# Tying the woven projections and the score products to each other in the third attention unit

## The chip, the cores and the metric

The kernel runs on one core of one Trainium2 chip. The metric is the device time of one execution in microseconds (us). It is given as the median of three executions; the profile is of one further execution.

## The reference, cut to what matters

The reference is a two-layer diffusion backbone over 1024 latent tokens (a grid 64 wide) and 256 context tokens, 1024 features wide. The even layer, in which the change lies, projects the normalised tokens to queries, keys, values and gates, and attends in two groups of eight heads with two key heads each:

```python
for i in range(DEPTH):                      # DEPTH = 2
    h_lat = rms_norm(x_lat, norm_g[i]) * (1 + sc_l) + sh_l      # h_ctx likewise
    if i % 2 == 0:
        # A: all 1280 keys, normalised q and k, rotary;  B: keys within 128 and the context, a sink
        oa, ob = softmax(qa @ ka.T) @ va, softmax(qb @ kb.T + band) @ vb
        y_lat = concat([oa * silu(ag), ob * silu(bg)]) @ w_out
    else:
        y_lat = ...                         # convolution and neighbourhood attention
    x_lat = x_lat + g_l * y_lat
return rms_norm(x_lat, final_g)
```

## The kernel before, in words

Every product is kept near 32-bit accuracy by splitting both operands into a high and a low part: `mm3` (L317) makes three matmuls of one, high by high, high by low and low by high, and leaves the last of them in `done[0]` (L315). Weights are loaded raw, cast to their high part on ScalarE (ACT) and subtracted to their low part on GpSimd (POOL) in `load_w` (L324); the loads are issued by SyncE (SP), two raw buffers deep.

The attention of the even layer is cut into four **units** of one key head and four query heads. `ORDER` (L76) runs them as 2, 3, 0, 1: two of group B with 42 tiles each, then two of group A with 84 each. A unit has ten blocks of 128 queries, in the order `QORD`; a **tile** is one block against 128 keys. The generator `attn_gen` (L392) makes the tiles of all units one after the other, in two steps a tile. The first step traces two score products `st` (L465 with the queries' high part, L469 with the low part and the row maxima), an exponential `pf` on ACT (L477), its cast `ph` on ACT and the rest `pl` on POOL or VectorE (DVE) (L296, L299). The second flushes the tile three before: three products `ov` with the values (L409 to L411). Scores have two PSUM banks and `pf` two buffers. Before a block's first tile can be completed, its row maxima are needed: products `mx` (L576, L588) that DVE reduces (L578, L589), a transpose `trn` (L387) and the write of `QL` (L388). The high part of a unit's keys comes back from DRAM (`KAt`, L551) and ACT copies it into the lower operand (`KBt`, L555).

Beside the attention of one unit runs the projection of the next. `fill0` (L865) gives the query, key and value products `pq` of `proj_qkv` (L789): ten blocks of 128 tokens, eight feature blocks of three matmuls with 384 columns each. It yields after feature blocks 1, 4 and 7, so that one **step** is six or nine matmuls. A block's result is copied from PSUM to `pc` on ACT (L802); two blocks share a `pc` buffer, of which there are three (`PCB`). Normalisation and rotary follow on ACT, DVE and POOL, and `qk_tail` (L834) transposes the result (`trk`, L838) and writes queries and keys to DRAM. A tail is taken up with a later block, or in one of the last four steps. `proj_gate` (L767) then makes the gate products `pg`, six results in eighteen steps. It uses the same eight weight buffers as `pq`, and its results the same two PSUM banks. The products `po` of the output projection (L1003) are the work beside the fourth unit; their inputs and weights need buffers that the gate products read last.

`weave` (L495) draws the two strands together. It takes one step of `main` after the other and, in proportion, the steps of `fill`. What it traces is not the order on the chip: a scheduler orders every engine's instructions by a timeline of its own, taking what is ready there and, among that, the lowest priority number. A fill step is traced with its number raised by 80 (`FL`, L502). With `lag`, every TensorE instruction of the step gets an edge behind an earlier score product, the one at `sts[-lag]` (L503): an edge of `issue_after` fixes the order on that one engine and adds no wait for the result. The order so found is fixed on the chip.

The third unit is loop index `k = 2` in L883 to L890. Its 168 main steps are woven in two calls: 120 steps with 34 steps of `fill0(3)` (30 of `pq` and four of tails), then 48 steps with 18 of `proj_gate`. In the kernel before, `lag` is used in the odd layer alone (L1505 to L1512).

Of the kernel before, what the change touches and what calls it, by code (L numbers as in the profile page):

```python
# [49 lines left out]
NLAST = (48, 28)  # L50
# [16 lines left out]
ENDS = ((0, 0, 512), (1, 0, 256), (1, 256, 256))  # L67
LATE = 100
NFILL = (34, 34, 34)
HV = (('gggvvvvg',) * 3, ('gggvvvvg', 'vvvgvvvg', 'gggvvvvg'))  # L70
O1 = (6, 84, 46, 14)
TICK0, TICK1 = (1, 3)
# [3 lines left out]
ORDER = (2, 3, 0, 1)  # L76
# [11 lines left out]
def tile_kernel(ctx: ExitStack, tc: tile.TileContext, a, out):  # L88
    nc = tc.nc
    VE, SC, GP, PE, SY = nc.vector, nc.scalar, nc.gpsimd, nc.tensor, nc.sync  # L90
# [8 lines left out]
    turn = [0, 0]  # L99
    mk, mwp, hold, layer = [0], [None], [0], [0]  # L100
    sts, pvs = [], []

    def bank(tag, name):
        if tag == "pp" and solo[0]:
            turn[0] += 1
            tag = ("pp", "mx")[turn[0] // 2 % 2]
        return ps.tile([P, 512], F32, tag=tag, name=name, bufs=BUFS[tag])
# [3 lines left out]
    def nm(s):  # L111
        uid[0] += 1
        return f"{s}_{uid[0]}"
# [187 lines left out]
    def make_h(l, c, xs, bc, h):  # L301

        cond = 1 if c == 0 else 0
        for dk in range(DK):
            x = xs(dk)
            VE.scalar_tensor_tensor(x, x, gs[l][:, dk, cond : cond + 1], bc, op0=ALU.mult, op1=ALU.mult)
            shift = modT[l][:, dk, cond : cond + 1]
            if HV[l][c][dk] == "v":
                SC.activation(h[0][:, dk, :], x, AF.Identity, bias=shift)
# [2 lines left out]
                SC.activation(x, x, AF.Identity, bias=shift)  # L312
                split(x, h[0][:, dk, :], h[1][:, dk, :])

    done = [None]  # L315

    def mm3(o, lh, ll, rh, rl, first, last):  # L317
        PE.matmul(o, lh, rh, start=first, stop=False)  # L318
# [73 lines left out]
    def attn_gen(pool, groups, vshare, look, nexts=None):  # L392
# [43 lines left out]
        def prepare(x, n):  # L436

            while n and work and work[0][0] <= x:
                if next(work[0][1], work) is work:
                    work.pop(0)  # L440
                else:
                    n -= 1
# [7 lines left out]
        for x, (g, t) in enumerate(items):  # L450
            if x + AHEAD < len(items):
                items[x + AHEAD][0].ahead(items[x + AHEAD][1])
            if t == 0:
                g.start()
                while any(p is g.prep for _, p in work):
                    prepare(len(items), 1)
                for k in g.ids:
                    next(preps[k])
                    work.append((x + LEAD[layer[0]], preps[k]))
            rate = g.rate * max(len(work), 1)  # L460
            k, q0, n, extra = g.tiles[t]
            KA, KB = g.k()
            st = bank("st", nm("st"))
            cs = slice(k * P, (k + 1) * P)
            sts.append(PE.matmul(st[:, :n], KA[:, cs], g.QH[:, q0 : q0 + n], start=True, stop=False))  # L465
            if not g.bias:
                for lhs, rhs in extra():
                    PE.matmul(st[:, :n], lhs, rhs, start=False, stop=False)
            PE.matmul(st[:, :n], KB[0:68, cs], g.QL[0:68, q0 : q0 + n], start=False, stop=True)  # L469
            ph = pool.tile([P, 512], F32R, tag="ph", name=nm("ph"), bufs=look + 1)  # L470
            pl = pool.tile([P, 512], F32R, tag="pl", name=nm("pl"), bufs=look + 1)
            pf = pool.tile([P, 512], F32, tag="pf" if layer[0] else "ost", name=nm("pf"), bufs=PFB)
            if g.bias and extra is not None:
                VE.tensor_tensor(pf[:, :n], st[:, :n], extra(), op=ALU.add)
                SC.activation(pf[:, :n], pf[:, :n], AF.Exp)
            else:
                SC.activation(pf[:, :n], st[:, :n], AF.Exp, scale=1.0 if g.bias else SCALE)  # L477
            cnt[0] += 1
            split(pf[:, :n], ph[:, :n], pl[:, :n], "s", "v" if cnt[0] % vshare == 0 else "g")
            pend.append((g, t, ph, pl))  # L480
            if t == len(g.tiles) // 2:
                g.gate()
            if t == len(g.tiles) - 1:
                g.last()
            prepare(x, rate // 2)
            yield
            if len(pend) > look:
                flush()
            prepare(x, rate - rate // 2)
            yield  # L490
# [1 line left out]
            flush()  # L492
            yield

    def weave(main, nmain, fill, nfill, last=True, all_fill=True, lag=0):  # L495

        done = 0
        for k in range(nmain):
            next(main, None)
            while done * nmain < (k + 1) * nfill:  # L500
                with ExitStack() as cx:
                    cx.enter_context(later(FL[layer[0]]))  # L502
                    if lag and len(sts) >= lag:  # L503
                        cx.enter_context(tc.issue_after(sts[-lag].ins))
                    next(fill, None)
                done += 1
        if all_fill:
            for _ in fill:
                pass
        if last:  # L510
            for _ in main:
                pass
# [139 lines left out]
    with ExitStack() as p0x:  # L652
# [114 lines left out]
        def proj_gate(u, ms):  # L767

            if u not in gw:
                gw[u] = load_g0(u) if u == ORDER[0] else load_w0("ev_g", u, 256)  # L770
            wh, wl = gw[u]
            for m, c in ms:
                t0, n = CHUNKS[c]
                pp = bank("pp", nm("pg"))
                for dk in range(DK):
                    ms_ = slice(m * P, (m + 1) * P)
                    mm3(pp[:, :n], wh[dk][:, ms_], wl[dk][:, ms_], Hs(h, 0, t0, n, dk), Hs(h, 1, t0, n, dk),
                        dk == 0, dk == DK - 1)
                    if dk % 3 == 1:
                        tick()  # L780
                        yield
                sg = ap.tile([P, 640], F32, tag="rt2", name=nm("sg"), bufs=2)
                silu2(pp[:, :n], sg[:, :n])
                mark[0] = SY.dma_start(Gs[u][:, m, t0 : t0 + n], sg[:, :n])
                for _ in range(2):
                    if tails:
                        qk_tail(*tails.pop(0))
# [71 lines left out]
        def gblocks(k):  # L859

            if k:
                return [], [(m, c) for c in range(3) for m in range(2)]
            return [(0, c) for c in range(3)], [(1, c) for c in range(3)]

        def fill0(k, w=None):  # L865
            yield from proj_qkv(ORDER[k], w)
            while tails and k:
                qk_tail(*tails.pop(0))
                yield
            yield from proj_gate(ORDER[k], gblocks(k)[0])  # L870
# [11 lines left out]
        main = attn_gen(a0, [group0(u, qb) for u in ORDER for qb in QORD], VS0, LOOK0)  # L882
        for k in range(3):  # L883
            u = ORDER[k]
            n = NSTEP[u // 2] + (12 if k == 0 else 0)
            n0 = 0 if k else N0
            if not k:
                weave(main, n0, proj_gate(u, gblocks(k)[1]), 9, False)
            weave(main, n - n0 - NLAST[u // 2], fill0(k + 1), NFILL[k], False)
            weave(main, NLAST[u // 2], proj_gate(ORDER[k + 1], gblocks(k + 1)[1]), 18, False)  # L890
        run(mods)


# [205 lines left out]
    with ExitStack():  # L1099
# [404 lines left out]
        main = attn_gen(dpool, groups1, VSH, LOOK1, {11: [], 12: [13, 14], 13: [15]})  # L1504
# [129 lines left out]
```

## Time and profile before

| what | value |
| --- | --- |
| median of three executions | 1556.66 us (1556.37 to 1558.11) |
| profiled execution, its own time | 1555.72 us |
| its span, first to last instruction | 1553.9 us |
| TensorE (PE) busy | 1449.1 us, 93% of the span |
| VectorE (DVE), GpSimd (POOL), ScalarE (ACT) busy | 1123.3, 833.5, 759.8 us |
| mean granted TensorE clock | 0.967 |

The span leaves out 1.8 us of the execution's own time that lie around it. In the profile's rows a line number like L465 is one of the kernel's source, names like `pq<-wh,hh` are the tile written and the tiles read, and PE stands for TensorE's matmuls, PEld for its weight loads. Matmuls are pipelined: one of 384 columns is shown with 0.34 us, though the next one starts sooner, so neighbouring rows overlap. A row's bracket gives the idle time of the engine before it and what ended it. In a table by stretches of time each row has the stretch, its length, the busy time and count of each engine, the granted clock, and the share and rate of the DMA engines.

### The profile page before, as it was taken

The numbers are of one execution on the slowest core, as the hardware profiler recorded it, in microseconds if no ns is written. First come the engines' busy times: TensorE is split into PE (matmuls) and PEld (weight loads), VectorE is DVE, ScalarE is ACT, GpSimd is POOL, SyncE is SP. The second block draws the span as 40 slices with busy tenths as digits, with TensorE's granted clock in tenths as the row PEclk, the third lists the DMA queues.
The fourth block names the chain that finished last, engine by engine and source line by source line (L and its number), as shares of the span: only waits on it lengthen the run. The fifth ranks groups of instructions, "written<-read, shape, count | busy, mean of one in ns | idle before, by whom it ended". The sixth has DMA issues, their size and how long they took to land.

```text
span 1553.9 us, 22052 instructions
## 1 busy us (share of the span) xinstructions
PE 1449.1 (93%) x6984; PEld 1172.3 (75%) x6984; DVE 1123.3 (72%) x2172; ACT 759.8 (49%) x1545; POOL 833.5 (54%) x762
## 2 busy tenths in 40 slices
PE   6989989999999989899999889999999999799995
PEld 1878868887789678678887668888787787687784
DVE  4998898689858666654577677999755457586776
ACT  2721354445454755565455555443434455545563
POOL 1561464555555676675455666664542443545574
PEclk9999999999999999999999999999999999899996
DMA  9548245423441124631111121213456888788623
GB/s 339 194 146 270 79 125 174 147 64 121 151 129 44 54 89 143 207 115 56 42 45 35 68 95 57 80 63 123 158 178 222 272 225 263 221 264 240 192 92 109
DMA packets 185614, 221.01 MB, mean 142 GB/s; under 512 B 17421, under 2 KB 139481, under 8 KB 185497
## 3 DMA queue, kind: packets, MB, share of 16 engines
q1 hardware_dynamic: 178832, 208.03, 43.1%
q10 hardware_dynamic: 6664, 11.57, 2.3%
q8 instruction: 55, 0.90, 0.2%
q14 instruction: 63, 0.51, 0.1%
HBM read 159.51 MB, written 60.03 MB: 141 GB/s over the span
## 4 chain that ended last, share of the span: by engine, by line
PE 67%; DVE 12%; DMA 11%; issue 3%; POOL 3%; ACT 2%; SPq 2%; DVEq 0%; ACTq 0%; POOLq 0%
PE p L320 6%; PE p L318 6%; PE p L319 6%; PE ov L409 4%; PE ov L410 4%; PE ov L411 4%; PE st L465 4%; PE po L318 4%; PE st L469 4%; PE po L319 4%; PE po L320 4%; PE pq L320 2%; PE pq L319 2%; PE pq L318 2%; DMA mw<-in_mod_w_dram 2%
## 5 line engine op out<-in xcount | busy, mean ns | idle before, releaser
L299 POOL TENSOR_TENSOR pl<-pf,ph 128x512 fp32r<-128x512 f32 (+4 forms) x321 | 399.9, 1258 | 270.7 <-ACT ph L296 218.9
L299 POOL TENSOR_TENSOR wl<-wr,wh 128x256 fp32r<-128x256 f32 (+2 forms) x256 | 197.7, 788 | 227.9 <-ACT wh L296 203.3
L477 ACT ACTIVATE pf<-st 128x512 f32<-128x512 f32 x284 | 166.2, 596 | 161.7 <-PE st L469 106.3
L296 ACT CAST ph<-pf 128x512 fp32r<-128x512 f32 (+4 forms) x364 | 209.2, 588 | 25.5 <-PE ov L410 17.6
L296 ACT CAST wh<-wr 128x256 fp32r<-128x256 f32 (+2 forms) x264 | 103.2, 404 | 172.2 <-DMA wr<-in_od_d_dram 39.3
L318 PE MATMUL p<-hh,wh 128*128 128x512 f32 x448 | 177.7, 399 | 3.7 <-DVE spk L299 1.4
L319 PE MATMUL p<-hl,wh 128*128 128x512 f32 x448 | 177.9, 398 | 0.2 <-POOL hl L299 0.2
L320 PE MATMUL p<-hh,wl 128*128 128x512 f32 x448 | 175.2, 399 | 0.1
L465 PE MATMUL st<-QH,KAt 128*128 128x512 f32 (+4 forms) x364 | 144.0, 397 | 19.8 <-ACT pf L477 16.5
L409 PE MATMUL ov<-ph,Vt 128*128 128x512 f32 (+4 forms) x364 | 143.6, 394 | 8.8 <-DVE y L631 6.4
L411 PE MATMUL ov<-pl,Vt 128*128 128x512 f32 (+4 forms) x364 | 143.7, 395 | 3.9 <-POOL pl L299 3.8
L410 PE MATMUL ov<-ph,Vt 128*64 128x512 f32 (+4 forms) x364 | 140.8, 387 | 0.0
L469 PE MATMUL st<-QL,KBt 68*128 68x512 f32 (+4 forms) x364 | 138.2, 388 | 0.8 <-DVE QL L388 0.7
L1116 DVE SCALAR_TENSOR_TENSOR cps<-U,taps,cps 128x512 f32<-128x512 f32 x184 | 124.3, 747 | 0.0
L589 DVE TENSOR_REDUCE mp<-mx 128x1 f32<-128x512 f32 x128 | 85.5, 682 | 33.5 <-PE mx L588 32.7
L219 DVE SCALAR_TENSOR_TENSOR macc<-mw,csil,macc 128x512 f32<-128x512 f32 x107 | 97.5, 929 | 14.0 <-DMA mw<-in_mod_w_dram 13.2
L318 PEld LDWEIGHTS p<-hh,wh 128*128 128x128 f32 x448 | 84.6, 189 | 24.5 <-DVE spk L299 1.6
L465 PEld LDWEIGHTS st<-QH,KAt 128*128 128x128 f32 x364 | 69.8, 192 | 42.5 <-ACT pf L477 25.3
L319 PEld LDWEIGHTS p<-hl,wh 128*128 128x128 f32 x448 | 84.6, 189 | 20.4 <-POOL hl L299 0.6
L320 PEld LDWEIGHTS p<-hh,wl 128*128 128x128 f32 x448 | 84.6, 189 | 20.3 <-POOL wl L299 1.0
L411 PEld LDWEIGHTS ov<-pl,Vt 128*128 128x128 f32 x364 | 71.1, 195 | 28.1 <-POOL pl L299 7.6
L409 PEld LDWEIGHTS ov<-ph,Vt 128*128 128x128 f32 x364 | 71.5, 196 | 24.3 <-issue 7.0
(277 smaller groups left out, 3518.4 us busy)
## 6 DMA issues: line engine op xcount, KB each, us to landing
mw<-in_mod_w_dram SPq DMA_DIRECT2D x34, 512.0 KB, 5.6
bs<-in_d_bs_dram SPq DMA_DIRECT2D x16, 832.0 KB, 7.3
Q<-qs SPq DMA_DIRECT2D x40, 256.0 KB, 2.7
QH<-Q SPq DMA_DIRECT2D x80, 128.0 KB, 2.7
bm<-in_d_bm_dram SPq DMA_DIRECT2D x16, 540.0 KB, 6.1
wr<-in_od_d_dram SPq DMA_DIRECT2D x64, 128.0 KB, 2.6
mw<-in_mod_w_dram SPq DMA_DIRECT2D x28, 256.0 KB, 3.1
wr<-in_ev_qkv_dram SPq DMA_DIRECT2D x32, 192.0 KB, 3.8
```

Source lines behind the costliest of these rows:

```text
L296: SC.copy(hi, src)
L299: (GP if leng == "g" else VE).tensor_tensor(lo, src, hi.bitcast(F32), op=ALU.subtract)
L318: PE.matmul(o, lh, rh, start=first, stop=False)
L319: PE.matmul(o, lh, rl, start=False, stop=False)
L320: done[0] = PE.matmul(o, ll, rh, start=False, stop=last)
L409: PE.matmul(o, V[:, 64:192], ph[:, :n], start=(t == 0), stop=False)
L410: PE.matmul(g.ov[0:64, q0 : q0 + n], V[:, 0:64], ph[:, :n], start=False, stop=False)
L411: pvs.append(PE.matmul(o, V[:, 64:192], pl[:, :n], start=False, stop=(last and g.sink is None)))
L465: sts.append(PE.matmul(st[:, :n], KA[:, cs], g.QH[:, q0 : q0 + n], start=True, stop=False))
L469: PE.matmul(st[:, :n], KB[0:68, cs], g.QL[0:68, q0 : q0 + n], start=False, stop=True)
L477: SC.activation(pf[:, :n], st[:, :n], AF.Exp, scale=1.0 if g.bias else SCALE)
L1116: VE.scalar_tensor_tensor(pc, uc, w, pc, op0=ALU.mult, op1=ALU.add)
```

## The change

In the third unit alone, both calls of `weave` get `lag=4` and a new `tie=2`. With `lag`, every PE instruction of a fill step is ordered behind the fourth-last score product traced so far. With `tie`, `weave` notes after each fill step the last `mm3` product traced (`prods` is another name for the list `done`, since `done` is a local counter in `weave`), and the L465 product of the next tile is ordered behind the product noted two fill steps back in the same call. No operation, buffer or transfer is added or removed.

```diff
+HOLD, TIE = 4, 2
...
+    tied = [None]
...
-    done = [None]
+    done = prods = [None]
...
-            sts.append(PE.matmul(st[:, :n], KA[:, cs], g.QH[:, q0 : q0 + n], start=True, stop=False))
+            with ExitStack() as cx:
+                if tied[0] is not None:
+                    cx.enter_context(tc.issue_after(tied[0].ins))
+                sts.append(PE.matmul(st[:, :n], KA[:, cs], g.QH[:, q0 : q0 + n], start=True, stop=False))
...
-    def weave(main, nmain, fill, nfill, last=True, all_fill=True, lag=0):
+    def weave(main, nmain, fill, nfill, last=True, all_fill=True, lag=0, tie=0):
 
         done = 0
+        past = []
         for k in range(nmain):
+            tied[0] = past[-tie] if tie and len(past) >= tie else None
             next(main, None)
+            tied[0] = None
             while done * nmain < (k + 1) * nfill:
                 with ExitStack() as cx:
                     cx.enter_context(later(FL[layer[0]]))
                     if lag and len(sts) >= lag:
                         cx.enter_context(tc.issue_after(sts[-lag].ins))
                     next(fill, None)
+                past.append(prods[0])
                 done += 1
...
-            weave(main, n - n0 - NLAST[u // 2], fill0(k + 1), NFILL[k], False)
-            weave(main, NLAST[u // 2], proj_gate(ORDER[k + 1], gblocks(k + 1)[1]), 18, False)
+            hold = dict(lag=HOLD, tie=TIE) if k == 2 else {}
+            weave(main, n - n0 - NLAST[u // 2], fill0(k + 1), NFILL[k], False, **hold)
+            weave(main, NLAST[u // 2], proj_gate(ORDER[k + 1], gblocks(k + 1)[1]), 18, False, **hold)
```

## The prediction

> **What bounds the kernel now.** The page comes first: which engine is busy, and whose work makes up the chain that ended last.
>
> ```profile
> span 1553.9 us, 22052 instructions
> ...
> PE 1449.1 (93%) x6984; PEld 1172.3 (75%) x6984; DVE 1123.3 (72%) x2172; ACT 759.8 (49%) x1545; POOL 833.5 (54%) x762
> ...
> PE 67%; DVE 12%; DMA 11%; issue 3%; POOL 3%; ACT 2%; SPq 2%; DVEq 0%; ACTq 0%; POOLq 0%
> ```
>
> PE leads both. The change takes no work from it, so it can win only where PE stands idle or runs at a lower clock. I therefore asked for a table by stretches from the end of the second unit's gate products to late in the fourth unit, cut where the products beside the attention begin or stop. The figures are the stretch, its length, the busy time of PE, PEld, DVE, ACT and POOL, the clock and the DMA share.
>
> ```profile
> core 0: us, PE busy (x) PEld busy (x) DVE busy (x) ACT busy (x) POOL busy (x), PEclk, DMA share, GB/s
> 437.20:485.10 47.90, 47.23 (x247) 41.69 (x247) 31.02 (x60) 24.27 (x47) 27.45 (x22) 1.00 0.30 95
> 485.10:503.00 17.90, 17.90 (x92) 15.95 (x92) 15.93 (x23) 10.56 (x19) 13.39 (x10) 1.00 0.12 37
> 503.00:544.50 41.50, 37.95 (x166) 26.64 (x165) 25.39 (x49) 29.14 (x52) 28.79 (x23) 1.00 0.17 54
> 544.50:556.00 11.50, 11.50 (x63) 10.84 (x63) 9.57 (x18) 5.67 (x12) 9.99 (x9) 1.00 0.26 85
> 556.00:580.20 24.20, 19.35 (x75) 13.50 (x74) 13.95 (x27) 13.97 (x28) 15.25 (x14) 0.86 0.27 80
> 580.20:640.00 59.80, 59.80 (x297) 48.46 (x296) 40.29 (x71) 34.29 (x62) 40.82 (x29) 1.00 0.44 136
> 640.00:669.40 29.40, 23.53 (x92) 16.16 (x91) 18.39 (x35) 18.93 (x33) 20.21 (x16) 0.94 0.89 281
> 690.00:860.00 170.00, 169.88 (x809) 136.80 (x808) 109.92 (x198) 85.37 (x162) 94.35 (x81) 1.00 0.16 48
> ```
>
> I call the first stretch A, the third B, the fifth C and the seventh D. PE idles 0.67 us in A, 3.55 in B, 4.85 in C and 5.87 in D, and not at all in the others before D. The clock costs at most 24.20 x 0.14 = 3.4 us in C and 29.40 x 0.06 = 1.8 in D. About 20 us are thus open. The last row is the pattern to reach: with `po` products mixed in, PE is idle for 0.12 of 170 us. The same stretches for tile `pq` alone (first figure: PE) tell why B is not like that:
>
> ```profile
> 437.20:485.10 47.90, 28.07 (x136) 23.99 (x136) 2.38 (x5) 1.00 0.30 95
> 485.10:503.00 17.90, 11.18 (x53) 9.41 (x52) 0.49 (x1) 1.00 0.12 37
> 503.00:544.50 41.50, 1.07 (x5) 0.91 (x5) 0.86 (x2) 1.00 0.17 54
> 544.50:556.00 11.50, 9.36 (x48) 8.35 (x48) 0.00 (x0) 1.00 0.26 85
> ```
>
> Most of the 240 `pq` matmuls run before 503; then 41 us of attention stand alone.
>
> **The change part by part.** *The hold moves `pq` out of A.* First, how far it runs ahead now: the L465 row for the time up to 471.3 and for 437.2 to 471.3, and three PE rows.
>
> ```profile
> L465 PE MATMUL st<-QH,KAt x84: 388/396/792, 159.4 to 470.3; 128*128 128x512 f32 x84
> ```
>
> ```profile
> L465 PE MATMUL st<-QH,KAt x12: 388/394/496, 442.2 to 470.3; 128*128 128x512 f32 x12
> ```
>
> ```profile
> 437.26 0.34 PE L318 MATMUL pq<-wh,hc 128*128 128x384 f32 x1
> 437.44 0.34 PE L319 MATMUL pq<-wl,hc 128*128 128x384 f32 x1
> ```
>
> ```profile
> 485.11 0.62 PE L469 MATMUL st<-QL,KBt 68*128 68x512 f32 x2
> ```
>
> Two units have 84 tiles, so the third unit's scores begin after 470.3 and its first two are completed at 485.11; `pq` starts at 437.26, ahead of 12 more scores of the second unit. With the change, step f of 34 is traced at main step 120f/34 and ordered behind the score four back: steps 0, 1, 2, 3 behind tiles -3, -2, 0, 2 of the unit. With two score banks, tile 2's product needs tile 0 completed. So at most steps 0 to 2, 24 matmuls, can run in A; 112 leave it. At the start-to-start time of 0.175 us (0.34 is a pipelined duration) that is 19.6 us of PE work, and 47.23 - 19.6 = 27.6 us remain. Does anything else hold A open? The unit's keys must arrive (ACT's row) and its maxima be reduced (tile `mp`, 449 to 478, DVE first):
>
> ```profile
> 448.48 1.26 ACT L555 CAST KBt<-KAt 64x1280 fp32r<-64x1280 f32 x1 [2.86 <-DMA KAt<-K]
> ```
>
> ```profile
> 449.00:478.00 29.00, 6.95 (x11) 0.00 (x0) 1.00 0.23 73
> ```
>
> The copy ends 12.5 us into A and the reductions need 7: 19.5 us, under the 27.6 of work. But in its fixed order ACT waits 2.86 us for that DMA with the exponentials queued behind, and `pq` covers this today. The nearest rows for attention alone are B, idle for 3.55/41.50 = 8.6%, a piece of the second unit, 2.90/28.00 = 10.4%, and C, 20%, where ACT also waits for a DMA:
>
> ```profile
> 344.00:372.00 28.00, 25.10 (x115) 17.54 (x114) 25.45 (x61) 17.81 (x41) 15.25 (x13) 1.00 0.31 92
> ```
>
> I take C's share: 5.5 us, so **+4.8** beside the 0.67 of now, and D's clock loss, **+1.8**. The ends are -0.7 (no idle left) and +19.6 (A as long as now).
>
> ```profile
> PE st L465 <- ACT pf L477: 1.2, 2, 0.8
> ```
>
> Here a rule of the Trainium skill can be weighed. C's clock fell after a hole of 2.19 us (row below), B's 3.55 us in smaller pieces (those of L465: 1.2 us in two) left it at 1.00. The Trainium skill, "TensorE: Matmul & The Clock Gate", Part 1, says that the clock halves after a window of about 3.4 us without work. By that rule A's short waits would cost no clock and the sum below would be 1.8 us lower; the trace's hole was shorter than that window and the clock fell.
>
> *The same matmuls fill B: **-3.6**.* From the third unit's start a step of 1.05 or 1.6 us (six or nine times 0.175) goes with every 1.76 tiles, and the tie keeps it from falling more than two steps behind, as in the row 690 to 860. What `pq` results cost elsewhere comes along: on tile `pc`, DVE, ACT and POOL work for 10.28, 5.67 and 3.77 us between 437.2 and 503.
>
> ```profile
> 437.20:503.00 65.80, 0.49 (x3) 0.39 (x3) 10.28 (x12) 5.67 (x12) 3.77 (x5) 1.00 0.25 79
> ```
>
> Even all of it on top of B's 25.39, 29.14 and 28.79 stays below B's length, which the moved `pq` makes longer still; the writes of queries, keys and values go with it on SP, behind which the next loads queue, and I count nothing for them. Lower and upper end: -3.6 and 0.
>
> *C.* PE, then ACT, in C; below, the same hand-over in the first and second unit:
>
> ```profile
> 560.61 0.50 PE L465 MATMUL st<-QH,KAt 128*128 128x512 f32 x1 [2.19 <-ACT pf L477]
> ...
> 572.77 0.49 PE L838 MATMUL trk<-ident,pc 128*128 128x128 f32 x3
> ...
> 580.21 0.28 PE L318 MATMUL pg<-hc,wh 128*128 128x256 f32 x1
> ```
>
> ```profile
> 559.14 0.40 ACT L296 CAST wh<-wr 128x256 fp32r<-128x256 f32 x1 [4.23 <-DMA wr<-in_ev_g_dram]
> ...
> 568.48 0.41 ACT L296 CAST wh<-wr 128x256 fp32r<-128x256 f32 x1 [0.62 <-DMA wr<-in_ev_g_dram]
> ...
> 577.80 0.88 ACT L802 COPY pc<-pq 128x384 f32<-128x384 f32 x2
> ```
>
> ```profile
> 225.00:238.00 13.00, 10.64 (x45) 7.55 (x44) 11.33 (x29) 10.01 (x28) 9.04 (x10) 0.87 0.51 159
> 384.00:394.00 10.00, 7.98 (x39) 5.74 (x39) 9.82 (x18) 5.29 (x15) 5.72 (x6) 1.00 0.41 123
> ```
>
> The last two `pq` blocks are finished by 556, but copied only at 577.80, after a tail's transposes at 572.77: they wait for a `pc` buffer, and the gate, which needs their banks, starts at 580.21. Its weights were ready by 568.9. Spread out, `pq` ends behind tile 48 and before 53, its tails in step with it, and the gate starts from tile 57 on. What then remains is the weight loading, as in the earlier hand-overs: 2.36 us idle with 1.7 of clock, and 2.02 idle; 3 in the middle. From 4.85 + 3.4 to 3: **-5.2**, with ends 0 and -8.2. The ties add an order, no semaphore: if the gate's weights are late, the score of tile 62 and every `mx` and `ov` behind it wait in PE's queue. From 556 to 568.9 the loads took 13 us; nine tiles lie between, at B's 41.50/24 = 1.73 us (48 score products, two a tile) 15.6 us. I take nothing; if that cover goes, up to 4.
>
> ```profile
> 503.00:544.50 41.50, 15.59 (x48) 8.48 (x48) 0.00 (x0) 13.76 (x23) 1.00 0.17 54
> ```
>
> *D.* The last gate step moves behind tile 79 of 84, so the loads that wait for the gate's buffers and fill D (DMA share 0.89) come at the fourth unit's start. I let the hole move with them. The fourth unit's keys come with tails that are now over before the gate begins, so ACT's wait for them goes: **-2.1**. Ends: -7.7 (all of D covered) and +5.5 (the loads add a hole like A's to the unit's start).
>
> ```profile
> 649.77 1.27 ACT L555 CAST KBt<-KAt 64x1280 fp32r<-64x1280 f32 x1 [2.06 <-DMA KAt<-K]
> ```
>
> **Sum:** 4.8 + 1.8 - 3.6 - 5.2 - 2.1 = -4.3 us on the profiled execution's own 1555.72 (1.8 us around the span stay). The median, 1556.66, lies 0.9 above; there it is **1552.4 us**. About 0.2%, 3.1 us, can be told from no change: 1553.5 and 1559.8 are the borders.
>
> **The rivals.** *Slower: A becomes a hole.* Everything rests on the third unit's first scores coming as soon as PE is free. If instead the keys' DMA, the maxima on DVE and ACT's fixed order set the pace, PE stands still with the fills held back. B, C and D give back 10.9; with 1.8 of clock that is spent when A's idle time reaches 0.67 + 9.1 = 9.8 us, that is when the first L469 of the unit comes 37.4 us after the second unit's last `pg`. At 42 us it is 14.4 idle and 3.4 of clock: +17.1 - 10.9 = +6.2, **1562.9**. For it: the chain ends at 47.9 now. Against: the 28 us of `pq` on PE in A stand between its links.
>
> *No measurable change: C's hole stays.* If the weight loads alone make it, the 5.2 go: +0.9, **1557.6**. For it: the 4.23 us before an `ev_g` cast; against: the gate waited on past 568.9.
>
> *A larger gain: A is covered.* With B's share of idle time, 2.4 us, and no clock loss A costs 1.7: -9.2, **1547.5**. If D is covered as well, 5.6 less. Work left over for the end of the fourth unit's attention could add some of its 6.47:
>
> ```profile
> 880.00:900.00 20.00, 13.53 (x51) 9.30 (x49) 12.42 (x21) 13.26 (x24) 12.25 (x11) 0.83 0.01 3
> ```
>
> *It does nothing*: the order already keeps the bounds. The 12 scores after 437.26 exclude it nearly.
>
> **How the numbers follow.** Forecast 0.33, with a range of its own from 1549 to 1553.5; larger gain 0.17; C's hole stays 0.19; no effect 0.01; slower 0.30. Hence faster 0.50, same 0.20, slower 0.30. The range goes from 1543 (short of the case with D covered and work left over) to 1565 (a little past the slower case); under 0.1 is left out on either side. A at its full +19.6 is beyond it.
>
> **What would show it.** Right: the first third-unit `pq` stands behind the 82nd L465; A lasts under 37 us; B's tiles have `pq` between them and PE idles under 0.5 us there; the last two `pc` copies no longer come as a pair after a pause; the gate starts within 15 us of the last `pq`. Wrong: waits of `st` on `pf` or of `mx` on `mp` of several us before the 86th L465, a clock under 1.00 there, or `st` rows that follow a `pg` which waited for `wh`.

## The result, and the profile after

| what | before | after |
| --- | --- | --- |
| median | 1556.51 us (1555.31 to 1558.11, 4 runs) | 1575.84 us (1571.42 to 1577.32, 4 runs) |
| ratio | 1 | 1.0119 (95% interval 1.0097 to 1.0141) |
| profiled execution, its span | 1555.72, 1553.9 | 1577.32, 1575.5 |

The changed kernel is 1.2% **slower**. The forecast was 1552.4 us with a range of 1543 to 1565; the result lies outside it and on the other side of no change. A second measurement on another chip gave 1.0099 (1.0080 to 1.0117).

The page of the changed kernel, in the lines that were shown of before: the span, the engines, and the chain that ended last by engine.

```profile
span 1575.5 us, 22040 instructions
...
PE 1463.3 (93%) x6984; PEld 1180.9 (75%) x6984; DVE 1138.3 (72%) x2172; ACT 762.0 (48%) x1545; POOL 833.2 (53%) x762
...
PE 61%; DVE 14%; DMA 12%; issue 5%; POOL 3%; ACT 2%; SPq 1%; ACTq 0%; DVEq 0%; POOLq 0%
```

The counts behind the engines' names are those of before, yet PE is busy 14.2 us longer: 8.1 of it in the odd layer's attention, where the granted clock is 0.94 instead of 0.97, and 3.9 in the hand-over, which has ten products more (last and second rows of the two tables below). On the chain PE's share falls from 67 to 61%, with more DVE, issue and DMA.

To see where the 21.6 us of the two spans arose, cut both traces at the same five places: the end of the second unit's gate products, the last score product of layer 0, the first `p` product of the odd layer, and the first and last score product of the odd layer. Columns: the stretch, its length, busy time of PE, PEld, DVE, ACT, POOL, then clock, DMA share and rate. Before:

```profile
437.20:897.10 459.90, 439.69 (x2070) 350.58 (x2070) 297.83 (x532) 258.73 (x478) 290.62 (x235) 0.98 0.27 83
897.10:923.60 26.50, 21.13 (x100) 16.84 (x99) 21.66 (x38) 16.64 (x41) 18.78 (x21) 0.87 0.20 64
923.60:1213.30 289.70, 285.15 (x1315) 231.04 (x1314) 212.07 (x350) 121.15 (x237) 151.07 (x155) 1.00 0.41 132
1213.30:1516.30 303.00, 284.87 (x1388) 230.90 (x1387) 207.52 (x486) 166.33 (x353) 150.54 (x160) 0.97 0.75 220
```

After:

```profile
440.80:898.60 457.80, 439.57 (x2062) 349.52 (x2061) 302.42 (x525) 259.43 (x475) 288.77 (x234) 0.99 0.27 84
898.60:933.50 34.90, 25.02 (x110) 19.66 (x109) 28.54 (x45) 18.76 (x43) 18.96 (x24) 0.85 0.15 47
933.50:1224.80 291.30, 285.55 (x1315) 230.77 (x1314) 211.88 (x350) 120.95 (x236) 151.00 (x154) 1.00 0.41 132
1224.80:1538.00 313.20, 292.92 (x1386) 236.54 (x1385) 211.11 (x486) 164.56 (x351) 148.36 (x159) 0.94 0.74 213
```

Read the lengths down the column. Ahead of 437 us the changed kernel is 3.6 us later, in a part whose order is untouched; in the other traces the same mark lies between 436.6 and 444.7, so executions differ by that much without any change. The attention that the change edits is 2.1 us **shorter**. The hand-over to the next layer is 8.4 longer, the odd layer's projections 1.6, and the odd layer's attention **10.2**, where no edit stands. 3.6 - 2.1 + 8.4 + 1.6 + 10.2 is 21.7; behind it 0.1 comes back.

The edited part by stretches that answer to A, B, C and D of the prediction: A; up to the last `pq` in three pieces; the pause before the gate; the gate's first part; the start of the fourth unit's loads; the end of the attention. Left out (`...`) are stretches in which PE idles 0.13 us at most.

```profile
440.80:473.50 32.70, 27.89 (x123) 20.66 (x122) 20.94 (x37) 20.64 (x39) 21.54 (x18) 0.95 0.39 115
473.50:507.90 34.40, 34.37 (x166) 28.86 (x165) 25.88 (x44) 20.90 (x37) 20.43 (x16) 1.00 0.15 46
507.90:556.90 49.00, 46.01 (x221) 38.47 (x220) 36.62 (x59) 26.21 (x48) 31.02 (x25) 0.97 0.17 49
556.90:590.30 33.40, 32.62 (x161) 26.48 (x160) 29.41 (x50) 20.01 (x39) 23.93 (x20) 1.00 0.30 92
590.30:609.10 18.80, 15.92 (x61) 10.25 (x60) 14.39 (x24) 12.49 (x26) 14.39 (x13) 0.91 0.46 140
609.10:650.00 40.90, 38.83 (x194) 30.47 (x193) 27.53 (x53) 22.29 (x39) 24.98 (x20) 1.00 0.30 92
...
682.30:700.00 17.70, 13.17 (x57) 9.22 (x58) 12.22 (x22) 9.58 (x18) 12.61 (x10) 1.00 0.95 297
...
850.00:898.60 48.60, 48.60 (x230) 38.95 (x229) 30.31 (x55) 29.60 (x56) 30.96 (x26) 1.00 0.18 60
```

Length less PE's busy time is idle time; length times what the clock lacks is clock loss, an upper bound, since a low clock also falls on idle time. Before, the end of the attention was the one stretch not yet shown:

```profile
851.80:897.10 45.30, 40.15 (x179) 30.39 (x178) 29.58 (x50) 28.42 (x53) 29.24 (x24) 0.92 0.17 58
```

| stretch | idle + clock loss before | after | difference | forecast |
| --- | --- | --- | --- | --- |
| A, start of the third unit | 0.67 + 0 | 4.81 + 1.6 | +5.7 | +6.6 |
| B, up to the last `pq` | 3.55 + 0 | 0.03 + 2.99 + 0.78, + 1.5 | +1.8 | -3.6 |
| C, pause and gate | 4.85 + 3.4 | 2.88 + 2.07, + 1.7 | -1.6 | -5.2 |
| D, moved to the fourth unit's start | 5.87 + 1.8 | 4.53 + 0 | -3.1 | -2.1 |
| end of the attention | 5.15 + 3.6 | 0 | -8.8 | not in the sum |
| hand-over | 5.37 + 3.4 | 9.88 + 5.2 | +6.3 | not in the sum |

The rows A to D add to +2.8 where -4.3 was forecast. The first five rows add to -6.0, the length shows only -2.1. That is the idle time alone: PE is busy for 439.57 us of this part after and 439.69 before, so the 4.0 us of clock loss that the table takes away are not found in its busy time, and these rows don't say where they went. Attention and hand-over together, the whole edited stretch, grew from 486.4 to 492.7 us, by 6.3.

### The profile page after: what moved, and what is told of

The parts are those of the page before. It is cut to its first block, busy times and chain, and to the rows that moved or that the text cites. A ratio compares the mean times of both kernels' runs of the same rounds, so it can differ in the third digit from the quotient of the medians.

```text
span 1575.5 us, 22040 instructions
## 1 busy us (share of the span) xinstructions
PE 1463.3 (93%) x6984; PEld 1180.9 (75%) x6984; DVE 1138.3 (72%) x2172; ACT 762.0 (48%) x1545; POOL 833.2 (53%) x762
## 4 chain that ended last, share of the span: by engine, by line
PE 61%; DVE 14%; DMA 12%; issue 5%; POOL 3%; ACT 2%; SPq 1%; ACTq 0%; DVEq 0%; POOLq 0%
PE p L320 6%; PE p L321 6%; PE p L322 6%; PE ov L411 4%; PE st L470 3%; PE st L474 3%; PE ov L412 3%; DMA mw<-in_mod_w_dram 3%; PE ov L413 3%; PE po L320 3%; PE po L321 3%; PE po L322 3%; PE pq L322 2%; PE pq L320 2%; PE pq L321 2%
## 5 line engine op out<-in xcount | busy, mean ns | idle before, releaser
L322 PE MATMUL pq<-wh,hl 128*128 128x384 f32 x256 | 87.2, 343 | 0.7 <-DVE hl L312 0.7
```

The lines of the kernel that those rows point to most:

```text
L322: done[0] = PE.matmul(o, ll, rh, start=False, stop=last)
```

## The experiments

All ratios are to the kernel before, run beside it on the same chip; medians are of 5 to 12 runs (23 to 35 of the kernel before), intervals of 95%.

What the two sides of the binding do to the order can be read from the programs: the **tie alone** (`lag=0`) gives on every engine the order of before, instruction for instruction; the **hold alone** gives exactly the order of the changed kernel. All that follows is therefore about the hold. And the two orders, equal in the whole first half of the odd layer, differ again in the odd layer's attention (on PE from about 1300 us on), although no edge of the change reaches there. The scheduler found another order there; why is not shown.

**1. The hold in the first call only, and in the second only.**

```diff
-            weave(main, NLAST[u // 2], proj_gate(ORDER[k + 1], gblocks(k + 1)[1]), 18, False, **hold)
+            weave(main, NLAST[u // 2], proj_gate(ORDER[k + 1], gblocks(k + 1)[1]), 18, False)
```

> The new order is kept in the first woven call alone (the query, key and value products); the gate products are woven as before. Its order in the odd layer is nearly that of the kernel before. Theory 1 (late output projection: held-back gate products delay the output projection, and its rest stands alone behind the attention): the gate ends some 15 to 25 us earlier than in the changed kernel, the first po product starts at 655 to 672 instead of 689, the hand-over after the attention costs under 3 us, time 1553 to 1560. Theory 3 (the rival on record: the hold makes a hole at the third unit's start): that hole is still there, time 1570 or more.

Measured: 1.0004 (0.9983 to 1.0024). A is as in the changed kernel (27.89 us of work in 32.70, from 438.7 to 471.4), so its hole costs nothing in the end. The gate, now free, begins at 581.9, before the last `pq` at 589.9.

```profile
L320 PE MATMUL pg<-hc,wh x16: 277/280/285, 581.9 to 601.9; 128*128 128x256 f32 x16
```

The hand-over lasts 28.5 us with 5.5 of idle time, more than the 3 expected.

The mirror image removes `**hold` from the first call and keeps it in the second.

> The new order is kept in the second woven call alone (the gate products); the query, key and value products run ahead as before. Its order in the odd layer is that of the kernel before. Theory 1: the gate is held as in the changed kernel, po starts at 680 to 695, the hand-over costs 6 to 10 us, and the stretch from the end of pq at 556 to the first held gate product has no fill, time 1564 to 1572. Theory 3: nothing is moved at the unit's start, time 1555 to 1558.

Measured: 1.0014 (0.9994 to 1.0033), well below what was expected. The hand-over did grow, to 33.5 us, but the hole at the end of the attention went as well (48.60 busy of 48.60):

```profile
845.00:893.60 48.60, 48.60 (x230) 38.94 (x228) 30.32 (x55) 29.57 (x56) 30.90 (x26) 1.00 0.18 60
893.60:927.10 33.50, 25.03 (x109) 19.95 (x108) 28.62 (x45) 18.70 (x42) 19.06 (x24) 0.85 0.15 50
```

In both of these kernels the odd layer's attention has the order of before (in the first but for 38 rows). What follows: neither half of the hold alone costs the 1.0 to 1.2%. Nor do the halves add up within layer 0: from the end of the second unit's gate products to the first `p` the two traces show 484.4 and 486.5 us, before 486.4, but the four traces with the changed kernel's layer 0 show 491.9 to 494.0. A reading that fits is that each half is paid for out of the same hole at the end of the attention (8.8 us of idle time and clock loss before, about 4.5 with the first half, 0 with the second), which cannot pay for both; no run tests it.

**2. The odd layer's order set back, or put in by itself.** From the middle of the odd layer every engine's instructions are chained in the other kernel's order (`PIN`, one list of instructions for each engine), by edges that add no semaphore; layer 0 is left alone.

```diff
+        here = {i.name: i for i in tc.nc.cur_bb.bb.instructions}
+        for row in PIN:
+            names = [f"I-{n}" for n in row if f"I-{n}" in here]
+            for x, y in zip(names, names[1:]):
+                tc.add_manual_dep(here[y], x, mybir.DependencyInfo(mybir.DependencyClass.NoSync, mybir.DependencyReason.DATA),
+                                  reason="pin")
```

The changed kernel with the odd layer of before:

> The changed kernel, but from the middle of the odd layer on each engine's instructions are chained in exactly the order that they have in the kernel before. Theory 1 with theory 2 (the scheduler also reordered the odd layer, where the change has no edge, and that order is slower): the loss after 1300 us goes, the hand-over's stays, time 1563 to 1568. If the loss after 1300 us is not due to the order there: 1573 to 1577.

Measured: 1.0038 (1.0020 to 1.0057). The kernel before with the odd layer of the changed one:

> The kernel before, but from the middle of the odd layer on each engine's instructions are chained in exactly the order that they have in the changed kernel. Theory 2: 8 to 11 us slower than before, all of it after 1300 us, time 1564 to 1568. If that order costs nothing by itself: 1555 to 1558.

Measured: 1.0055 (1.0032 to 1.0077). In the traces the odd layer's attention lasts 299.1 us in the first of the two and 311.1 in the second. The two parts add to 0.93%; the whole change once more:

> The changed kernel once more, beside its pieces on one chip. Theory: 1.009 to 1.013, the sum of the two parts measured apart (about 0.4% to the odd layer, 0.55% from there on). Rival (the first four runs were an unlucky draw): 1.005 to 1.008.

Measured: 1.0099 (1.0080 to 1.0117). By the medians 0.55 to 0.61 of the 0.99%, more than half of the loss, are thus the order of a layer that the change doesn't touch; by the intervals the share could also be a third or three quarters.

**3. Two other kernels that fall into that odd-layer order by themselves.** One is that of point 5. The other: with `HOLD = 10` in the first call only, layer 0 differs from the changed kernel's, but from the odd layer's attention on the scheduler gives every engine the changed kernel's order (twelve rows of VectorE apart).

```diff
-HOLD, TIE = 4, 2
+HOLD, TIE = 10, 2
...
-            hold = dict(lag=HOLD, tie=TIE) if k == 2 else {}
+            hold = dict(lag=HOLD) if k == 2 else {}
...
-            weave(main, NLAST[u // 2], proj_gate(ORDER[k + 1], gblocks(k + 1)[1]), 18, False, **hold)
+            weave(main, NLAST[u // 2], proj_gate(ORDER[k + 1], gblocks(k + 1)[1]), 18, False)
```

> Hold of 10 scores, in the first weave call only, no tie. In layer 0 the pq begin half a unit into the gap and the gate is not held, but from the odd layer's attention on every engine has the order of the changed kernel, not that of before. Theory (the odd layer's order is a cost of its own, whatever put it there): ratio to before 1.003 to 1.006, of which 1.004 to 1.006 arise behind 1213 us and layer 0 gives back 0 to 3 us; score 363 comes 3 to 6 us later against score 252 than in before. Rival (the odd layer lost only because the run was late or by chance): ratio 0.998 to 1.001, and score 252 to score 363 takes 303 us as in before.

Measured: 1.0072 (1.0043 to 1.0100), a little above what was expected. Then once more, beside its partner with the odd layer chained as in before:

> The hold of 10 in the first call only, once more, with the odd layer's order of the changed kernel that it has by itself: ratio 1.005 to 1.009.

> The hold of 10 in the first call only; from the middle of the odd layer every engine in the order of before. Theory B: 0.4 to 0.7% less than its partner, 0.999 to 1.003. Rival (the hold of 10 is dear in layer 0 itself): within 0.2% of the partner.

Measured: 1.0055 (1.0026 to 1.0084) and **0.9989** (0.9971 to 1.0007). The only difference between the two is the odd layer's order. The score products there, from the first to the last of 112, with the hold of 10 and then its partner:

```profile
L470 PE MATMUL st<-QH,KAt x112: 262/388/775, 1225.4 to 1540.6; 128*128 128x512 f32 x48, 128*128 128x256 f32 x16, 128*128 128x352 f32 x16, 128*128 128x320 f32 x16
```

```profile
L478 PE MATMUL st<-QH,KAt x112: 264/386/775, 1220.8 to 1523.9; 128*128 128x512 f32 x48, 128*128 128x256 f32 x16, 128*128 128x352 f32 x16, 128*128 128x320 f32 x16
```

That is 315.2 against 303.1 us. (Both profiled executions were the slowest of their twelve, 1580.38 and 1563.12 us; the medians, 1565.21 and 1557.41, lie 7.8 us apart.) The longest waits of PE between them (total, times, longest), in the same sequence:

```profile
PE mx L1352 <- DMA QH<-QD: 6.4, 3, 3.4
PE mx L1352 <- DMA gt<-GD: 5.1, 1, 5.1
...
PE mx L1352 <- issue: 2.7, 1, 2.7
```

```profile
PE mx L1360 <- DVE pl L309: 3.0, 1, 3.0
...
PE mx L1360 <- DMA KAt<-KD: 1.8, 1, 1.8
PE mx L1360 <- DMA QH<-QD: 1.4, 1, 1.4
```

In this pair the products for the maxima wait longer for the next block's queries and gates. That is not so in every pair: their waits on transfers come to 3.2 to 12.3 us in the eleven traces with the order of before and to 4.4 to 14.8 in the six with the other, 7.3 in the kernel before and 7.2 in the changed one. What sets the orders apart in every trace is one wait on issue: 2.4 to 3.6 us in all seven with this order on TensorE; of the eleven with the order of before, one has 0.2 us of it and the others none. That is a part of the loss; what makes the rest is open. In the changed kernel itself the odd attention's 10.2 us are 2.15 of idle time and 8.05 of matmuls that took longer, at the lower clock. From the first to the last score the odd layer's attention lasts 299.1 to 306.7 us in the eleven traces with the order of before, and 304.7 to 319.2 in the six with all engines in the other; the one below 311 is that of point 5.

**4. Only the transfers set back.** Since those waits are for DMAs, SyncE alone was chained in the order of before; the other engines keep the changed kernel's.

> The changed kernel; from the middle of the odd layer SyncE alone issues its transfers in the order of before, while TensorE, VectorE, ScalarE and GpSimd keep the changed kernel's. The transfers run at 80 to 90% of the DMA engines there. Theory (the changed order of the loads is what costs, the compute engines follow them): ratio as with all engines set back, 1.002 to 1.006. Rival (the order on the compute engines costs): as the changed kernel, 1.009 to 1.013; mismatched orders of loads and use could make it worse still.

Measured: 1.0141 (1.0118 to 1.0163): worse than the change itself, so the theory that the loads' order alone is the cause falls. The odd layer's score products take 324.7 us in its trace (1223.6 to 1548.3). That loads and their use must be in step fits this, and is not tested further. Which engine's part of the order would be enough for the loss stays open; the opposite mix, loads in the changed order and the other engines in that of before, cannot run, since these two orders block each other.

**5. The hand-over: products held without the change.** In the changed kernel `po` starts late, because the gate is late. To hold `po` alone, the kernel before got a `lag` in its two calls for output products, first of 4, then of 3:

```diff
-        weave(main, O1[1], out0_part(parts[0]), 48, False)
-        weave(main, O1[2], chain(load_oh(parts[1]), out0_part(parts[1])), 30, False)
+        weave(main, O1[1], out0_part(parts[0]), 48, False, True, 4)
+        weave(main, O1[2], chain(load_oh(parts[1]), out0_part(parts[1])), 30, False, True, 4)
```

> The kernel before with nothing of the change in it; its output products beside the fourth unit's scores are held four scores back, so that 388 of them instead of 438 stand ahead of score 230 (378 in the changed kernel), and the odd layer has the order of before but for a few rows. Theory (work left over fills the hole at the attention's end, and the hand-over behind it gets dearer by as much): idle time and clock loss from score 230 to 251 shrink by 5 to 9 us, those from score 251 to the first p grow by 5 to 8, together within 3 us of before's 17.5; ratio 0.998 to 1.002. Rival (the hand-over grew in the changed kernel because the gate was held, not because of the po): hand-over as before, 26 to 28 us, and ratio 0.994 to 0.997.

Measured: 1.0015 (0.9995 to 1.0035). The hand-over stayed at 26.6 us; part of the hole at the end was filled. The expectation on the hand-over missed, and for a moment the gate seemed to be the cause. With the hold of 3:

> The kernel before, its output products held three scores back, nothing of the change in it: 474 instead of 492 of them ahead of score 245, as in the changed kernel. From the odd layer's attention on every engine has the order of the changed kernel, without any pin. Theory A (late po make the hand-over dear): score 251 to first p 32 to 36 us. Rival (the gate held back does it, not the po): 26 to 29. Theory B (the odd layer's order costs by itself): 6 to 10 us more behind 1213 us, ratio 1.005 to 1.009. Rival: 0.999 to 1.003.

> The same hold of three scores on the output products, and from the middle of the odd layer every engine in the order of before. Layer 0 as in its partner. Theory B: 0.4 to 0.6% less than its partner, 0.999 to 1.003. Rival (the order there doesn't matter): the same as the partner within 0.2%.

Measured: 1.0095 (1.0068 to 1.0122) and 1.0062 (1.0039 to 1.0084), both above what was expected. The end of the attention and the hand-over, with 4 and then with 3:

```profile
847.10:900.50 53.40, 50.51 (x232) 39.64 (x231) 34.57 (x58) 29.94 (x55) 33.59 (x28) 0.96 0.16 55
900.50:927.10 26.60, 23.09 (x101) 18.13 (x100) 23.37 (x41) 18.19 (x42) 16.55 (x21) 0.82 0.20 66
```

```profile
848.60:895.80 47.20, 47.20 (x223) 37.84 (x222) 29.56 (x53) 29.58 (x55) 31.45 (x26) 1.00 0.19 62
895.80:932.10 36.30, 26.47 (x110) 21.23 (x109) 29.25 (x47) 18.43 (x41) 18.38 (x26) 0.81 0.20 61
```

With neither `pq` nor gate touched, late output products alone make the hand-over 36.3 us long (36.6 in the partner): the theory holds, with a step in it. The step can be seen on DVE, where the first instructions that form the next layer's input (L306, L308 in the changed kernel) stand as one row of eight. Before and in the changed kernel:

```profile
894.05 5.36 DVE L306 SCALAR_TENSOR_TENSOR x<-x,gs,bc 128x512 f32<-128x512 f32 x8 [5.83 <-PE bc L261]
```

```profile
902.84 5.35 DVE L308 SCALAR_TENSOR_TENSOR x<-x,gs,bc 128x512 f32<-128x512 f32 x8 [1.25 <-PE bc L263]
```

Against the last score product (897.1 and 898.6) it begins 3.1 us before it and 4.2 us behind it; with `po` held by 4 it begins 1.1 us before it, by 3 5.2 us behind. All 18 traces fall into two groups. In eleven the block begins 1.1 to 3.2 us ahead of the last score, and the hand-over lasts 26.5 to 30.1 us; in seven (the second call's hold alone, the hold of 3 and its partner, and the four with the changed kernel's layer 0) it begins 4.2 to 5.5 us behind, and the hand-over lasts 33.5 to 36.6. In the seven this block of 5.4 us, and the norm ahead of it, stand on DVE just when the last tiles need it; that this is what makes the step is read from the waits, not from a run that moves the block alone. The kernel before waits in its hand-over almost only for `ov`, most of it on POOL:

```profile
L411 PE MATMUL ov<-pl,Vt 128*128 128x512 f32 x4 | 2.3, 578 | 3.6 <-POOL pl L299 3.6
```

The changed one waits about as long for `ov`, now on DVE, and besides for the norm (2.43 us) and for the last output products' input and bank (2.3 and 1.4). PE there, the wait on the norm and then three groups from 898.6 to 933.5 (busy, mean ns, idle before and what ended it):

```profile
901.64 0.60 PE L263 MATMUL bc<-ident,nr 128*128 128x128 f32 x3 [2.43 <-DVE nr L243]
```

```profile
L320 PE MATMUL po<-hh,wh 128*128 128x512 f32 x16 | 7.1, 470 | 2.3 <-ACT hh L298 2.3
...
L320 PE MATMUL po<-hc,wh 128*128 128x256 f32 x12 | 4.0, 334 | 1.4 <-DVE x L1016 1.4
...
L413 PE MATMUL ov<-pl,Vt 128*128 128x512 f32 x4 | 2.5, 632 | 3.3 <-DVE pl L301 3.3
```

The hold of 3 gives the changed kernel's odd-layer order by itself. Setting that order back saves 0.33% by the medians, under the 0.4 to 0.6 expected, and the two intervals overlap; in the two traces the odd attention lasts 304.7 and 305.9 us. This pair therefore doesn't confirm point 3. What it adds is that late output products alone, with the odd layer in the order of before, cost 0.62% (0.39 to 0.84).

**6. Longer holds.** With the hold in the first call only (diff as in point 3, other numbers), more `pq` stays in A; for both of these the odd layer has the order of before.

> Hold of 14 scores, in the first weave call only, no tie; the order of the odd layer is that of before. 48 pq matmuls stand in the gap before the third unit's scores, the others beside its tiles. Theory (the gap costs where pq leaves it, the middle of the unit gains what pq brings, the late po are what makes the hand-over dear): gap within 2 us of before, 1 to 3 us gained between score 103 and 120, gate before 590, hand-over from score 251 to the first p within 2 us of before's 26.5; ratio 0.997 to 1.000. Rival (moving the pq is a cost in itself): 1.001 to 1.004.

Measured: 1.0043 (1.0024 to 1.0063), a little above the rival's range. From the end of the second unit's gate products to the first `p` its trace shows 489.8 us (440.2 to 930.0) against 486.4 before, and 305.6 against 303.0 in the odd attention. Three traces with the hold of 10, of one order in layer 0, show 487.2 to 489.7 for the first of these, so its 3.4 us are hardly more than executions differ by. Why 14 is dearer than 10 (with the odd layer set back) or 20 is open.

> Hold of 20 scores, in the first weave call only, no tie; the order of the odd layer is that of before. 66 pq matmuls stand in the gap. Theory: the gap as in before (0 to 1 us more idle), B's idle time partly filled, gate soon after score 120; ratio 0.997 to 1.000. Rival (moving the pq is a cost in itself, growing with the number moved): 1.000 to 1.002, nearer to before than the hold of 14.

> Hold of 20 scores in the first weave call only, once more. Theory: no difference from before, 0.998 to 1.001, since the 6 us saved between scores 100 and 144 stand against the same sum given back at three places behind. Rival (a true gain): 0.996 to 0.998.

Measured: 0.9988 (0.9967 to 1.0010) and 0.9996 (0.9978 to 1.0014): no difference. The last kernel holds both calls, by 12, with the tie:

> Hold of 12 scores with the tie of 2, in both calls; the odd layer has the order of before, but only 12 po matmuls stand ahead of score 168 (before 50) and 408 ahead of score 230 (before 450). Theory (the gate held back pushes the po and with them chunk 1's final projection into the hand-over): hole at the end of the attention filled (3 to 5 us), hand-over from score 251 to the first p 31 to 35 us instead of 26.5, and no loss behind it; ratio 1.000 to 1.004. Rival (the whole loss is the odd layer's order and the hand-over's is noise): ratio 0.996 to 0.999.

Measured: 1.0008 (0.9988 to 1.0028). Its hand-over lasts 30.1 us (894.1 to 924.2), a little under the expected 31 to 35; nothing is lost behind it. None of the variants is faster than before by more than its measurement is uncertain.

## Why the prediction was wrong

By the medians the change costs 19.3 us. The terms A to D came to +2.8 us instead of -4.3, by B and C, and the two largest losses stand in places that had no term in the sum: the hand-over behind the attention, 8.4 us longer, and the odd layer's attention, 10.2.

**A was right in size, not in its reason.** The prediction let 24 `pq` matmuls and 27.6 us of work stay in A and charged 4.8 of idle time and 1.8 of clock; the trace has 27.89 us of work in 32.7 and 5.7 us more of idle time and clock loss. The prediction took the idle time from C's share because ACT waits for the keys' transfer, with the exponentials behind it. PE's waits from 440.8 to 473.5 are others for the most part, so the size is in part luck:

```profile
PE trm L227 <- DVE macc L221: 1.4, 1, 1.4
PE ov L413 <- POOL pl L301: 1.3, 2, 0.7
PE mx L597 <- DVE mp L598: 1.2, 2, 1.0
PE st L470 <- ACT pf L482: 0.8, 1, 0.8
```

The first `pq` stands where it was expected, behind the 82nd score product:

```profile
L470 PE MATMUL st<-QH,KAt x82: 387/396/795, 160.9 to 465.2; 128*128 128x512 f32 x82
```

```profile
465.65 0.34 PE L320 MATMUL pq<-wh,hc 128*128 128x384 f32 x1
```

The "slower" rival, A as a hole with nothing to do, did not come to pass: A fell under 37 us. The kernel is slower for reasons that this rival doesn't name.

**B failed** (-3.6 forecast, about +1.8 found). The fill now stands beside every tile, yet 2.99 us of waits remain and 1.5 of clock loss come with them. PE's two largest waits from 507.9 to 556.9, and below them two of before from 503 to 556:

```profile
PE mx L597 <- DVE mp L587: 1.4, 1, 1.4
PE st L470 <- ACT pf L482: 0.9, 2, 0.7
```

```profile
PE mx L576 <- DMA QH<-Q: 1.2, 2, 0.7
PE mx L588 <- DVE mp L589: 0.7, 1, 0.7
```

The waits on the next block's queries are gone; those of `st` on `pf` shrank only from 1.2 to 0.9, and the largest, on the maxima of the next block, doubled. So the step that failed is that fill beside every tile covers every wait. The prediction argued with shares of busy time: DVE's with the copies of `pc` "stays below B's length". It does, at 36.62/49.00 = 75% against 25.39/41.50 = 61% before; but PE takes its instructions in a fixed order, and a wait is covered only by as much fill as stands in front of the waiting product at that moment. That this, and the copies on DVE that delay the maxima, make the waits is argued, not shown.

**C failed** (-5.2 forecast, -1.6 found). The forecast left 3 us of idle time and clock loss where 2.88 + 1.7 stand in the pause alone, and 2.07 us more in the gate behind it. It had the places right: `pq` ends behind tile 48 of the unit (counted from 0), and the gate starts behind tile 57, the layer's 142nd score product. But these nine tiles took 18.7 us where 15 were expected, and tile 57 *is* what the gate waits for:

```profile
590.34 0.34 PE L322 MATMUL pq<-wh,hl 128*128 128x384 f32 x1
```

```profile
608.48 0.50 PE L470 MATMUL st<-QH,KAt 128*128 128x512 f32 x1 [0.18 <-ACT pf L482]
...
609.06 0.28 PE L320 MATMUL pg<-hc,wh 128*128 128x256 f32 x1
```

The last bank is copied by 593.1 and the last weights are ready at 599.6, both well ahead of 609.06, so neither the copies nor the weights make this pause; the hold itself does. The step that failed: the prediction put the 3 us that it left down to the weight loads, and gave the nine tiles without fill no idle time of their own, though attention alone was idle for 8.6% in its own row for B. With the gate free (point 1) it starts 8 us before `pq` ends.

**D was right in size.** The loads moved with the gate to the start of the fourth unit (DMA share 0.95 in 682.3 to 700), and the hole shrank by 3.1 where 2.1 were forecast. The unit's keys are now copied at 630.05, ahead of the hole, and `st` waits there for `pf` 1.4 us instead of 4.0, as the prediction argued; the wait of `po` on its weights grew from 1.1 to 2.1.

**Left out of the sum: what is behind the fourth unit.** "Work left over" was named, as an upside of some of 6.47 us. It came, -8.8, and was paid back at the hand-over, +6.3 in idle time and clock loss and +8.4 in length; this term was put at nothing. The prediction looked at the hole that late `po` fill, and not at what waits for the last of them: the chain of output product, norm and next layer's input.

**Left out altogether: the odd layer.** Its attention is 10.2 us longer in the profiled pair, and points 2 and 3 put 0.55 to 0.66% on its order alone (the pair of point 5, less clear, 0.33). Nothing in the profile of before could have shown it; the argument took for granted that an edit's effect ends where its edges end. Without this part the change measures 1.0038 (1.0020 to 1.0057), still slower: by that, about 1562.5 us, inside the range of 1543 to 1565. What in the odd layer's order costs the time stays open.

**The clock.** The prediction weighed the rule of the Trainium skill, "TensorE: Matmul & The Clock Gate", Part 1, that the clock halves after a window of about 3.4 us without work, and sided with the row of before. A shows the same as that row: the granted clock is 0.50 in 452.4 to 455.8, and in the 3.4 us ahead of it PE was busy for 1.78.

```profile
449.00:452.40 3.40, 1.78 (x11) 1.28 (x11) 2.40 (x2) 1.57 (x2) 1.89 (x2) 1.00 0.92 231
452.40:455.80 3.40, 3.40 (x12) 2.81 (x13) 1.46 (x3) 3.37 (x8) 2.51 (x3) 0.50 0.09 31
```

The longest single wait there is 1.36 us (of `trm` on `macc`). In the kernel before, C's fall has the same pattern: PE was busy for 1.68 us of the 3.4 ahead of it.

```profile
560.10:563.50 3.40, 1.68 (x6) 0.97 (x6) 3.39 (x8) 1.68 (x4) 3.40 (x4) 1.00 0.13 39
563.50:570.30 6.80, 6.16 (x15) 4.38 (x15) 2.06 (x5) 3.90 (x8) 4.50 (x7) 0.50 0.27 80
```

In both places a stretch of that length that was half idle was enough, and the 1.8 us were rightly charged. A threshold doesn't follow: from 556.7 to 560.1 PE was busy for 1.72 us, and the clock stayed at 1.00 behind it. The slow spell of A, 3.4 us, is as long as the window that the Trainium skill gives there.

## What to carry to other kernels

In a program whose order a scheduler works out, an edge in one place can turn the order in a far one: compare the order of every engine over the whole program, and when it differs where no edge stands, chain that part as it was and measure the two parts apart, before explaining anything. Work that is pushed back into a hole ahead of a serial hand-over fills the hole, but ask what waits for the last of that work: here 8.8 us of idle time and clock loss went at the attention's end and the hand-over grew by 8.4. Two halves of a change that each cost nothing measurable cost something together here, so measure the whole as well as the parts. A wait in a fixed order is covered only by the work that stands in front of it at that moment, so a share of idle time is no measure of what a spread-out fill will cover.

## What the runs showed that was not expected

- TensorE's granted clock halved for 3.4 us after a stretch of that length in which PE was busy for 1.78 us, with no single wait over 1.36 us.
- Putting only the transfers back into the faster kernel's order made the kernel slower still (1.0141 against 1.0099): the mixed order cost more than the slower order throughout.
- The hand-over has a step: 26.5 to 30.1 us with the next layer's first VectorE block 1.1 to 3.2 us ahead of the last score product, 33.5 to 36.6 with that block 4.2 to 5.5 us behind it, and no trace between.
- The hold in either call alone costs nothing that can be measured (1.0004 and 1.0014); in both it costs 0.38% with the odd layer in the order of before.
